# Convolution taps of a two-layer transformer block tied to the steps they are written between, and their shares of three stretches changed

## The chip, the cores and the metric

The kernel runs on one core of one Trainium2 chip. What counts is the device time of one launch in microseconds (us), the median of the runs. Line numbers (L1039) are those of the kernel before, unless a sentence says that they are of the changed kernel, where the same lines stand some 18 or 19 further down (L1039 is L1058 there).

## The reference

Two layers over 256 latent tokens and 256 context tokens of width 1024. Each layer: half a feed-forward step, four token mixers on one normalised input, merged by gates, and another half feed-forward step. The second layer updates the latent tokens alone (`update_ctx` is false), so its mixers' outputs have 256 tokens and not 512.

```python
def conv_module(u, conv_w, conv_b, ln_g, ln_b):           # branch B, 512 channels
    a, g = jnp.split(u, 2, axis=-1)
    y = a * jax.nn.sigmoid(g)
    y = lax.conv_general_dilated(y, conv_w[:, None, :], ..., feature_group_count=B_CH) + conv_b   # 31 taps
    return jax.nn.silu(layer_norm(y, ln_g, ln_b))

def merge(y_a, y_b, y_c, y_d, gate_logits, w_branch, w_out):
    y = jnp.stack([y_a, y_b, y_c, y_d], axis=2)
    proj = jnp.einsum('btnc,ncd->btnd', y, w_branch)
    g = jax.nn.sigmoid(gate_logits.reshape(gate_logits.shape[:2] + (N_BRANCH, D_MODEL)))
    return jnp.einsum('btnd,btnd->btd', g, proj) @ w_out

def token_mixing(n, nc, ...):
    aq, ak, av, bu, cq, ck, cv, du, gl = split_cols(n @ w_in)
    ...
    # A: attention with grouped keys, B: conv_module, C: attention as the difference of
    # two softmaxes per head, D: a two-dimensional Fourier transform
    y = merge(y_a, y_b, y_c, y_d, gl, w_branch, w_out)
```

## The kernel before

**Products.** All weights are fp32. Each product is made of three fp32r matmuls: a weight is cut into a high half (`hi`, rounded by ACT, L196) and a low half (`lo`, the difference, by DVE, L197), the activations likewise, and TensorE (PE) adds hi by high, hi by low and lo by high (`mm3`, L211 to L213; `mm3_rows` for products whose rows are tokens, L1355 to L1357 in the profile). Weights come in by DMA in chunks of 128x1024 (`raw`, three buffers), in the order in which the kernel asks for them, and the halves have three buffers each. PE is never without such work for long: the other engines must bring the halves and the activations in time.

**The mixing of a layer** is written as a list of main steps (most of them matmuls with weights) with side steps strewn between them. `spread(main, *sides)` (L95) runs the main steps in order and, behind each, as many steps of each side list as the share of the main steps' costs that is done. There are three such stretches, and then a closing one:

1. Fourier branch D, gates and projection of branch 3 (`gates_first`, which is `merge(3)`), channel block 2 of the convolution's input (`b_block(2)`), queries and keys of head 0 of branch C. Side steps: attention A (`side_a`), and the convolution taps up to `at1`.
2. Channel block 3 (`b_block(3)`), gates and projection of branch 0 (`merge(0)`). Side steps: the heads of branch C (`side_c`: scores, turn, norm, values, out), and the taps from `at1` to `at2`.
3. Gates and projection of branch 2 (`merge(2)`), which needs the heads of C. Side steps: the taps from `at2` on, and the convolution's end (`conv_tail`).
4. Gates and projection of branch 1, the convolution's (`merge(1)`), then the output projection.

**The taps.** The convolution has four blocks of 128 channels, each with a padded input `yp` and a sum `cv` (`cv0` to `cv3`). A block has 31 taps on DVE: the first sets `cv` (L1036), the other 30 each do cv = yp shifted * weight + cv (L1039). They stand in 44 side steps of up to three taps, eleven to a block (`nconv`). A tap handles 128x512 elements in the first layer (layer 0 below, `S` = 2), 128x256 in the second (layer 1, `S` = 1).

**The convolution's end** (`conv_tail`): the four sums added up (`cs`), PE's column mean of them (`cmean`, L1052), the mean subtracted on DVE (L1056), squares on ACT added on DVE, the root of the variance (`cln`: two small matmuls `cln_ps` with an ACT function between them), and for each block a product on DVE, a scaling on POOL (L1075), a tanh on ACT and the split into `yh` and `yl` (L237) that branch 1 multiplies.

**A branch's projection** (`b`) is multiplied by its gate on DVE (`bt`, L1386), and added to the running sum on POOL (`h`, L1388). The heads of branch C run on several engines in turn: PE scores, ACT exponentials, DVE sums and reciprocals (`stc`), the difference of the two softmaxes (`ec`, L1284), PE's turn of it (`tpc`, L1194), PE's values. The queries and keys of branch A pass a norm (`aq_w` on DVE, `aq_ps` on PE, L473 and L478).

**What sets the order.** Outside some regions with an order by hand, a scheduler sets each engine's order: it takes the instructions as they are written as a priority, and by its own model of durations puts an instruction onto an engine's queue when its data would be there. An instruction whose inputs are ready early may so stand far ahead of where it is written. The taps need only `yp`, the weights and their own `cv`, and DVE had room by that model: the taps of a block stand soon behind their `yp`, ahead of the steps between which they are written. On the queue, each engine then runs its instructions in that order. High and low halves of chunks have a higher priority than the rest (`high_priority`).

Of the kernel before, what the change touches and what calls it, by code (L numbers as in the profile page):

```python
# [24 lines left out]
TAPS = 31  # L25
# [66 lines left out]
    return 0.8 - 0.6 * math.exp(-0.3 * l)  # L92


def spread(main, *sides):  # L95

    total, at = sum(c for c, _ in main), 0.0
    done = [0] * len(sides)
    for c, step in main:
        step()  # L100
        at += c
        for i, side in enumerate(sides):
            upto = min(len(side), int(len(side) * at / total + 1e-6))
            for f in side[done[i]:upto]:
                f()
            done[i] = upto


def stepped(steps, costs):
# [18 lines left out]
class Build:  # L128
    def __init__(self, nc, tc, es, d):
        self.nc, self.tc, self.d = nc, tc, d  # L130
        self.order = []
        self.after = self.region = None
        self.level = False
        pool = lambda name, **kw: es.enter_context(tc.tile_pool(name=name, **kw))
        self.tiny = pool("tiny", bufs=1)
        self.fix = pool("fix", bufs=1)
        self.wp = pool("wp", bufs=3)
        self.tmp = pool("tmp", bufs=2)
        self.ps = pool("ps", bufs=1, space=PSUM)
        self.dram = pool("dram", bufs=1, space=bass.MemoryType.DRAM)  # L140
        f = self.fix
        for i in range(2):
            self.tiny.tile([128, 8], F32, tag="rs", name=f"rs{i}", bufs=2)
        self.tiny.tile([128, 1], F32, tag="warm", name="warm", bufs=1)
        self.lam = [f.tile([128, 4], F32, name=f"lam{l}") for l in range(L)]
        self.eps = f.tile([128, 1], F32, name="eps")
        self.small = f.tile([128, N_SMALL], F32, name="small")
        self.mod = [f.tile([128, 72, 2], F32, name=f"mod{l}") for l in range(L)]
        self.zero = f.tile([128, 32], F32, name="zero")[:, 0:1]
        self.const = f.tile([128, EARLY], F32, name="const")  # L150
        self.st = f.tile([128, DB, 32], F32, name="st")
        self.h = f.tile([128, DB, 2 * T], F32, name="h")
        self.nh = f.tile([128, DB, 2 * T], F32R, name="nh")
        self.nl = f.tile([128, DB, 2 * T], F32R, name="nl")

    def sm(self, *key):
        o, w = SMALL[key if len(key) > 1 else key[0]]
# [30 lines left out]
    def cut(self, r, low="vector", pool=None, bufs=3, into=None):  # L188
        i = len(self.order)
        with self.tc.high_priority():  # L190
            if into is None:
                hi, lo = ((pool or self.wp).tile([128, 8, 128], F32R, tag=n, name=f"{n}{i}", bufs=bufs) for n in ("hi", "lo"))
            else:
                hi, lo = (t.rearrange("p (a b) -> p a b", a=8) for t in into)
            hv, lv = (t.rearrange("p a b -> p (a b)") for t in (hi, lo))
            self.nc.scalar.activation(out=hv, in_=r, func=AF.Copy)  # L196
            getattr(self.nc, low).tensor_tensor(out=lv, in0=r, in1=hv.bitcast(F32), op=ALU.subtract)  # L197
        return Chunk(hi, lo)

    def chunk(self, desc):  # L200
# [775 lines left out]
    def mixing(self, l, closing):  # L976
# [5 lines left out]
        with self.tc.tile_pool(name=f"mix{l}", bufs=2) as mp:  # L982
# [48 lines left out]
            def taps(i, k0, k1):  # L1031
                o, yp = conv_out[i], pads[i]
                for k in range(k0, k1):
                    x, wk = yp[:, :, k:k + T], cw[:, i, k:k + 1]
                    if k == 0:
                        nc.vector.tensor_scalar(out=o, in0=x, scalar1=wk, scalar2=self.sm("conv_b", l)[:, i:i + 1],  # L1036
                                                op0=ALU.mult, op1=ALU.add)
                    else:
                        nc.vector.scalar_tensor_tensor(out=o, in0=x, scalar=wk, in1=o, op0=ALU.mult, op1=ALU.add)  # L1039
# [232 lines left out]
            def c_k(h):  # L1272
                p = win(C_K + 128 * h, 512, f"ck{h}")
                t = self.held(f"ckt{h}")
                nc.scalar.activation(out=t, in_=p, func=AF.Copy)
                rope(t)
                ck[h] = stack_k(t, f"ck{h}")
# [161 lines left out]
            def lagged(stages, extra):  # L1439
                side = []  # L1440
                lag = max(d for d, _ in stages)
                for i in range(n + lag):
                    side += extra.get(i, [])
                    for d, f in stages:
                        if 0 <= i - d < n:
# [5 lines left out]
                            {per * j - d: [lambda f=f, j=j: f(j)] for j in range(1, 4) for d, f in ((2, a_q), (1, a_q_turn))})  # L1451
            side_c = lagged([(3, c_out), (2, c_values), (2, c_norm), (1, c_turn), (0, c_scores)],
                            {per * h - 1: [lambda h=h: c_q(h), lambda h=h: c_k(h)] for h in range(1, 4)})
            conv = [lambda i=i, k=k: taps(i, k, min(k + 3, TAPS)) for i in range(4) for k in range(0, TAPS, 3)]
            nconv = len(conv) // 4
            conv_tail = [conv_sum, conv_mean, conv_rstd, conv_turn] + [lambda i=i: conv_norm(i) for i in range(4)]
            turn = a_k()
# [18 lines left out]
            def b_block(i):  # L1476
                return [(8, lambda: b_gate(i)), (8, lambda: b_value(i))]
# [6 lines left out]
            else:  # L1484
# [2 lines left out]
                cover = [lambda g=g: (f_columns(g + 1), steps[g]()) for g in range(3)] + [steps[3]]  # L1487
                gates_first.insert(2, gates_first.pop(0))
            fourier = [(8, lambda: f_columns(0))] + [four(g, cover[g]) for g in range(4)]
            at1, at2 = 2 * nconv + 2, 3 * nconv  # L1490
            spread(fourier + gates_first[:6] + b_block(2) + gates_first[6:] + [(8, lambda: c_q(0)), (8, lambda: c_k(0))],
                   side_a, conv[:at1])
            spread(b_block(3) + merge(0), side_c, conv[at1:at2])
            spread(merge(2), conv[at2:] + conv_tail)
            ready = []

            def cut_first(i):
# [119 lines left out]
```

## Time and profile before

| | us |
|---|---|
| runs | 2226.83, 2226.89, 2227.34: median 2226.89 |
| profiled execution, by its own clock | 2227.85 |
| its span in the profile | 2226.1 |
| granted TensorE clock, mean | 0.997 |
| POOL busy | 92.1 |

The profile is of one execution. Its span is what the rows below are parts of; the execution's own time is 1.75 us longer than the span, the median of the runs 0.8 us longer. Stretches of the span are named by their start and end in us. The two mixings' parts with taps are 417 to 870 (layer 0) and 1705 to 1990 (layer 1).

### The profile page before, as it was taken

How to read it: one execution, taken by the hardware profiler on the slowest of the kernel's cores; microseconds unless marked ns; L12 is line 12 of the kernel's file. 1: busy time of each engine (PE TensorE's matmuls, PEld its weight loads, DVE VectorE, ACT ScalarE, POOL GpSimd, SP SyncE). 2: the span in 40 equal slices, each digit the busy share in tenths (PEclk: the TensorE clock that was granted, in tenths of full speed). 3: DMA queues.
4: the chain of work that ended last, by engine and by line, in shares of the span. 5: the costliest groups of instructions: out<-in, count | busy, mean ns of one | idle time of the engine just before them, and what ended most of it. 6: DMA issues, size and time to landing. Idle time of an engine off the chain costs nothing. (4 is left out here: it accounts for less than half of the span.)

```text
span 2226.1 us, 30137 instructions
## 1 busy us (share of the span) xinstructions
PE 2194.1 (99%) x11700; PEld 1855.1 (83%) x11700; DVE 1486.3 (67%) x2456; ACT 995.0 (45%) x1611; POOL 92.1 (4%) x96
## 2 busy tenths in 40 slices
PE   7999999999999999999999999999999999999998
PEld 6888889888887788898888898888889987779887
DVE  5787775794779646555656545565647969877665
ACT  5322223466556634433222233332224778756553
POOL 0000000100000113010000010000001000020000
PEclk9999999999999999999999999999999999999999
DMA  8566664322222222424544423544543433465554
GB/s 330 188 202 200 204 210 137 118 72 67 76 73 71 82 98 95 133 97 160 157 158 149 168 97 124 169 151 162 167 144 137 133 124 107 139 220 167 191 181 151
DMA packets 90815, 323.15 MB, mean 145 GB/s; under 512 B 9904, under 2 KB 12208, under 8 KB 90032
## 3 DMA queue, kind: packets, MB, share of 16 engines
q1 hardware_dynamic: 90672, 321.22, 43.3%
q8 instruction: 92, 1.51, 0.3%
q14 instruction: 51, 0.42, 0.1%
HBM read 315.94 MB, written 5.24 MB: 144 GB/s over the span
## 5 line engine op out<-in xcount | busy, mean ns | idle before, releaser
L196 ACT ACTIVATE hi<-raw 128x1024 fp32r<-128x1024 f32 x419 | 443.4, 1059 | 796.4 <-PE p L212 239.0
L197 DVE TENSOR_TENSOR lo<-raw,hi 128x1024 fp32r<-128x1024 f32 x416 | 518.7, 1247 | 245.6 <-ACT hi L196 239.8
L424 DVE SCALAR_TENSOR_TENSOR prods<-raw,cond 128x1024 f32<-128x1024 f32 x240 | 288.9, 1222 | 229.5 <-DMA raw<-wst 229.4
L211 PE MATMUL p<-nh,hi 128*128 128x512 f32 (+1 forms) x1040 | 398.0, 383 | 0.0
L212 PE MATMUL p<-nl,hi 128*128 128x512 f32 (+1 forms) x1040 | 397.8, 383 | 0.0
L213 PE MATMUL p<-nh,lo 128*128 128x512 f32 (+1 forms) x1040 | 397.8, 382 | 0.0
L212 PEld LDWEIGHTS p<-nl,hi 128*128 128x128 f32 x1040 | 195.5, 188 | 38.2
L211 PEld LDWEIGHTS p<-nh,hi 128*128 128x128 f32 x1040 | 195.4, 188 | 38.2
L213 PEld LDWEIGHTS p<-nh,lo 128*128 128x128 f32 x1040 | 195.5, 188 | 37.5
L213 PE MATMUL pr<-gh,lo 128*128 128x512 f32 (+1 forms) x480 | 177.8, 370 | 0.0
L212 PE MATMUL pr<-gl,hi 128*128 128x512 f32 (+1 forms) x480 | 177.8, 370 | 0.0
L211 PE MATMUL pr<-gh,hi 128*128 128x512 f32 (+1 forms) x480 | 177.8, 370 | 0.0
L1039 DVE SCALAR_TENSOR_TENSOR cv<-yp,cw,cv 128x512 f32<-128x512 f32 (+1 forms) x240 | 148.1, 617 | 4.6
L219 PE MATMUL p<-nh,hi 128*128 128x512 f32 x304 | 107.5, 397 | 0.1
L211 PEld LDWEIGHTS pr<-gh,hi 128*128 128x128 f32 x480 | 90.4, 188 | 15.7
L213 PEld LDWEIGHTS pr<-gh,lo 128*128 128x128 f32 x480 | 90.4, 188 | 15.5
L212 PEld LDWEIGHTS pr<-gl,hi 128*128 128x128 f32 x480 | 90.4, 188 | 15.4
L211 PE MATMUL g<-nh,hi 128*128 128x512 f32 x256 | 101.2, 396 | 0.0
L213 PE MATMUL g<-nh,lo 128*128 128x512 f32 x256 | 100.4, 392 | 0.0
L212 PE MATMUL g<-nl,hi 128*128 128x512 f32 x256 | 100.1, 391 | 0.0
L233 ACT ACTIVATE gh<-s 128x512 fp32r<-128x512 f32 (+1 forms) x88 | 50.6, 575 | 97.7 <-DVE s L773 92.5
L220 PE MATMUL p<-nh,lo 128*128 128x256 f32 x304 | 85.5, 281 | 0.0
(510 smaller groups left out, 4164.5 us busy)
## 6 DMA issues: line engine op xcount, KB each, us to landing
raw<-wst SPq DMA_DIRECT2D x556, 512.0 KB, 3.4
adaraw<-wst SPq DMA_DIRECT2D x4, 2048.0 KB, 19.0
adaraw<-wst SPq DMA_DIRECT2D x8, 512.0 KB, 6.2
cond<-cond SPq DMA_DIRECT2D x3, 1024.0 KB, 6.1
h<-h SPq DMA_DIRECT2D x4, 512.0 KB, 5.3
parked<-h SPq DMA_DIRECT2D x8, 256.0 KB, 4.3
h<-parked SPq DMA_DIRECT2D x8, 256.0 KB, 3.5
late<-late SPq DMA_DIRECT2D x2, 608.0 KB, 5.8
```

The costliest lines, as they stand in the source:

```text
L196: self.nc.scalar.activation(out=hv, in_=r, func=AF.Copy)
L197: getattr(self.nc, low).tensor_tensor(out=lv, in0=r, in1=hv.bitcast(F32), op=ALU.subtract)
L211: mm(out, w[0], x[0], start=start, stop=False)
L212: mm(out, w[0], x[1], start=False, stop=False)
L213: mm(out, w[1], x[0], start=False, stop=stop)
L219: mm(out, w[0], self.nh[:, k], start=start, stop=False)
L220: mm(out[:, CTX], w[1], self.nh[:, k, LAT], start=False, stop=stop)
L233: nc.scalar.activation(out=hi, in_=src, func=AF.Copy, scale=scale)
L424: nc.vector.scalar_tensor_tensor(out=products[:, s], in0=r, scalar=1.0, in1=cond[:, s], op0=ALU.mult, op1=ALU.mult, accum_out=self.mod[l][ ...
L1039: nc.vector.scalar_tensor_tensor(out=o, in0=x, scalar=wk, in1=o, op0=ALU.mult, op1=ALU.add)
```

## The change

`spread` gets a callback, `then`, which runs behind each main step and its side steps. In the mixing it is `mark`: it notes the DVE instruction written last (low halves of chunks left aside, which are kept in `cuts`). Each side step of taps is now `held`: the first DVE instruction that it issues, its first tap, gets a dependency on the mark before the last, so that the scheduler may not put it ahead of that instruction on DVE's queue. Both stand on one engine, so the dependency makes no semaphore and no wait; it binds the scheduler alone. Taps behind the first of a block follow it by their own data.

The shares change too. Layer 0: `at1` stays at 24 steps, `at2` goes from 33 to 29, so that four more steps of taps are written in the third stretch. Layer 1: `at1` and `at2` are both 33, so that three blocks' taps are written in the first stretch and none in the second; the last block's eleven steps stay in the third. Eight empty steps (`late`) stand ahead of the taps in the first stretch, so that they begin later, and `b_block(2)`, whose output the third block's taps need, is written behind three of branch 3's remaining gate and projection steps, not six (`nb`).

```diff
-def spread(main, *sides):
+def spread(main, *sides, then=lambda: None):
...
             for f in side[done[i]:upto]:
                 f()
             done[i] = upto
+        then()
...
+    def mark(self):
+
+        for i in reversed(self.nc.cur_bb.bb.instructions):
+            if i.engine == E.DVE and i.name not in self.cuts:
+                return i
+
+    def behind(self, step, mark):
+
+        at = len(self.nc.cur_bb.bb.instructions)
+        step()
+        for i in self.nc.cur_bb.bb.instructions[at:]:
+            if i.engine == E.DVE:
+                kind = mybir.DependencyInfo(mybir.DependencyClass.NoSync, mybir.DependencyReason.DATA)
+                self.tc.add_manual_dep(i, mark.name, kind, reason="behind")
+                return
...
-            conv = [lambda i=i, k=k: taps(i, k, min(k + 3, TAPS)) for i in range(4) for k in range(0, TAPS, 3)]
+            marks = []
+
+            def held(i, k):
+
+                self.behind(lambda: taps(i, k, min(k + 3, TAPS)), marks[-2])
+
+            conv = [lambda i=i, k=k: held(i, k) for i in range(4) for k in range(0, TAPS, 3)]
+            mark = lambda: marks.append(self.mark())
...
-            at1, at2 = 2 * nconv + 2, 3 * nconv
-            spread(fourier + gates_first[:6] + b_block(2) + gates_first[6:] + [(8, lambda: c_q(0)), (8, lambda: c_k(0))],
-                   side_a, conv[:at1])
-            spread(b_block(3) + merge(0), side_c, conv[at1:at2])
-            spread(merge(2), conv[at2:] + conv_tail)
+            at1, at2 = (2 * nconv + 2, 2 * nconv + 7) if S == 2 else (3 * nconv, 3 * nconv)
+            late = [lambda: None] * (0 if S == 2 else 8)
+            nb = 6 if S == 2 else 3
+            mark()
+            mark()
+            spread(fourier + gates_first[:nb] + b_block(2) + gates_first[nb:] + [(8, lambda: c_q(0)), (8, lambda: c_k(0))],
+                   side_a, late + conv[:at1], then=mark)
+            spread(b_block(3) + merge(0), side_c, conv[at1:at2], then=mark)
+            spread(merge(2), conv[at2:] + conv_tail, then=mark)
```

Every engine issues the same computation as before; only places on the queues differ. A new order on DVE also shifts what the scheduler does on the other engines. Three places follow, as the two programs order them. In these rows L1181, L1039 and so on are lines of the program that the fence shows, and a number behind a name tells one buffer from another.

DVE, layer 1, second stretch: the chain of a head of branch C (`stc` the sums and reciprocals, `ec` the difference of the softmaxes, `lam` its factor, `lo` a chunk's low half). Before:

```order
L1181 TENSOR_REDUCE stc_15582<-sc_15579 128x1
L1181 TENSOR_REDUCE stc_15590<-sc_15587 128x1
L1039 SCALAR_TENSOR_TENSOR cv_13513<-yp_15229,cw,cv_13513 128x256
L1185 RECIPROCAL stc_15582<-stc_15582 128x1
L1039 SCALAR_TENSOR_TENSOR cv_13513<-yp_15229,cw,cv_13513 128x256
L1185 RECIPROCAL stc_15590<-stc_15590 128x1
L1039 SCALAR_TENSOR_TENSOR cv_13513<-yp_15229,cw,cv_13513 128x256
L1282 TENSOR_TENSOR stc_15590<-stc_15590,lam_76 128x1
L1039 SCALAR_TENSOR_TENSOR cv_13513<-yp_15229,cw,cv_13513 128x256 x2
L197 TENSOR_TENSOR lo_15769<-raw_15766,hi_15768 128x1024
L1284 SCALAR_TENSOR_TENSOR ec_15584<-ec_15584,stc_15582,ec_15592 128x512
```

Changed:

```order
L1200 TENSOR_REDUCE stc_15598<-sc_15595 128x1
L1200 TENSOR_REDUCE stc_15606<-sc_15603 128x1
L1204 RECIPROCAL stc_15598<-stc_15598 128x1
L1204 RECIPROCAL stc_15606<-stc_15606 128x1
L1301 TENSOR_TENSOR stc_15606<-stc_15606,lam_76 128x1
L215 TENSOR_TENSOR lo_15779<-raw_15776,hi_15778 128x1024
L1303 SCALAR_TENSOR_TENSOR ec_15600<-ec_15600,stc_15598,ec_15608 128x512
```

The five taps between the head's steps are gone. Of the 124 taps of layer 1, 93 now stand in the first stretch, none in the second and the last block's 31 in the third; there they stand in groups of one to six between the low halves, where before there was no tap.

DVE, layer 0, third stretch (`bt` a projection times its gate). Before:

```order
L1333 SCALAR_TENSOR_TENSOR bt_6792<-gt_6693,b_6779 128x512
L1333 SCALAR_TENSOR_TENSOR bt_6808<-gt_6729,b_6795 128x512
L197 TENSOR_TENSOR lo_6895<-raw_6892,hi_6894 128x1024
L197 TENSOR_TENSOR lo_6937<-raw_6934,hi_6936 128x1024
L197 TENSOR_TENSOR lo_6974<-raw_6971,hi_6973 128x1024
L1333 SCALAR_TENSOR_TENSOR bt_6911<-gt_6768,b_6898 128x512
L1333 SCALAR_TENSOR_TENSOR bt_6927<-gt_6848,b_6914 128x512
```

Changed:

```order
L1352 SCALAR_TENSOR_TENSOR bt_6783<-gt_6683,b_6770 128x512
L1058 SCALAR_TENSOR_TENSOR cv_3256<-yp_5428,cw,cv_3256 128x512 x3
L1352 SCALAR_TENSOR_TENSOR bt_6799<-gt_6719,b_6786 128x512
L215 TENSOR_TENSOR lo_6889<-raw_6886,hi_6888 128x1024
L1058 SCALAR_TENSOR_TENSOR cv_3256<-yp_5428,cw,cv_3256 128x512 x6
L215 TENSOR_TENSOR lo_6933<-raw_6930,hi_6932 128x1024
L1058 SCALAR_TENSOR_TENSOR cv_3256<-yp_5428,cw,cv_3256 128x512 x6
L215 TENSOR_TENSOR lo_6970<-raw_6967,hi_6969 128x1024
L1058 SCALAR_TENSOR_TENSOR cv_3256<-yp_5428,cw,cv_3256 128x512
L1352 SCALAR_TENSOR_TENSOR bt_6905<-gt_6758,b_6892 128x512
```

41 taps now stand in this stretch between its low halves and its `bt` steps. Further ahead in layer 0, the taps of block 0 no longer stand within the chain of the query norm (`aq`), but behind it.

PE, layer 1, the end of the third stretch and the start of the fourth (`g` the products of a gate, `b` of a branch, `ada` small products of the next step's modulation). Before, where branch 1 begins:

```order
L1356 MATMUL g_16354<-lo_16425,nh 128x512
L1357 MATMUL g_16354<-hi_16424,nl 128x512
L1355 MATMUL b_16461<-hi_16451,yh_16311 128x512
L1356 MATMUL b_16461<-lo_16452,yh_16311 128x512
L1357 MATMUL b_16461<-hi_16451,yl_16312 128x512
```

Changed, from the mean on, with the rows between left out of the second part:

```order
L1374 MATMUL g_16493<-hi_16497,nh 128x512
L1071 MATMUL cmean<-cs,const 128x256
L1374 MATMUL g_16494<-hi_16497,nh 128x512
L1375 MATMUL g_16493<-lo_16498,nh 128x512
L1376 MATMUL g_16493<-hi_16497,nl 128x512
```

```order
L421 MATMUL ada_16391<-adaraw_16396,st 32x256 x4
L421 MATMUL ada_16391<-adaraw_16402,st 32x256 x4
L1374 MATMUL g_16493<-hi_16545,nh 128x512
L1374 MATMUL g_16494<-hi_16545,nh 128x512
L1374 MATMUL b_16461<-hi_16451,yh_16311 128x512
L1375 MATMUL b_16461<-lo_16452,yh_16311 128x512
L1374 MATMUL b_16477<-hi_16451,yh_16311 128x512
L1375 MATMUL b_16477<-lo_16452,yh_16311 128x512
```

The mean stood 89 of PE's instructions ahead of the first product of branch 1, and stands 34 ahead now; in PE's queue it has moved 84 instructions back. Behind the mean, up to the product that reads the last block's `yh` or `yl`, stand 42 matmuls of 128x512 and 24 small `ada` ones, and among them the two steps of `cln_ps`.

More of the change, by code (lines that the diff above doesn't have):

```diff
@@ L133, in __init__ @@
         self.level = False
+        self.cuts = set()
         pool = lambda name, **kw: es.enter_context(tc.tile_pool(name=name, **kw))
@@ L196, in cut @@
             self.nc.scalar.activation(out=hv, in_=r, func=AF.Copy)
-            getattr(self.nc, low).tensor_tensor(out=lv, in0=r, in1=hv.bitcast(F32), op=ALU.subtract)
+            i = getattr(self.nc, low).tensor_tensor(out=lv, in0=r, in1=hv.bitcast(F32), op=ALU.subtract)
+            self.cuts.add(i.ins.name)
         return Chunk(hi, lo)
```

## The prediction

> **What bounds the kernel now.** I read the page's busy times first, then busy times by stretch of the two mixings, then who TensorE waited for there.
>
> ```profile
> PE 2194.1 (99%) x11700; PEld 1855.1 (83%) x11700; DVE 1486.3 (67%) x2456; ACT 995.0 (45%) x1611; POOL 92.1 (4%) x96
> ```
>
> TensorE (PE) is busy for 2194.1 of the 2226.1 us span, so only 32 us can be won without taking matmuls away, and the change takes none. The next rows tell where part of the 32 us lies. Layer 0 (the first mixing) is 417 to 870 us, layer 1 (the second) 1705 to 1990.
>
> ```profile
> 417.00:480.00 63.00, 62.01 (x294) 50.85 (x293) 60.00 (x94) 29.41 (x50) 0.18 (x2) 1.00 0.25 84
> 640.00:710.00 70.00, 69.33 (x345) 57.10 (x344) 64.67 (x127) 42.69 (x86) 3.61 (x2) 1.00 0.22 73
> 710.00:750.00 40.00, 37.77 (x191) 31.24 (x190) 26.23 (x53) 25.46 (x49) 3.96 (x2) 1.00 0.21 71
> 750.00:832.00 82.00, 81.66 (x390) 66.56 (x389) 40.97 (x63) 38.66 (x70) 11.24 (x8) 1.00 0.28 97
> 1705.00:1760.00 55.00, 55.00 (x349) 49.58 (x348) 49.34 (x102) 35.16 (x57) 0.15 (x2) 1.00 0.41 135
> 1760.00:1845.00 85.00, 84.87 (x587) 72.36 (x586) 65.97 (x137) 66.29 (x130) 0.16 (x2) 1.00 0.36 118
> 1845.00:1920.00 75.00, 70.23 (x373) 58.25 (x372) 71.89 (x154) 56.98 (x96) 2.54 (x2) 1.00 0.36 120
> 1920.00:1957.00 37.00, 35.15 (x175) 28.35 (x174) 26.38 (x42) 28.57 (x48) 6.54 (x4) 1.00 0.43 143
> 1957.00:1990.00 33.00, 31.86 (x159) 23.42 (x157) 24.43 (x38) 21.09 (x31) 10.32 (x8) 1.00 0.65 219
> ```
>
> The columns are stretch, length, then busy time of PE, weight loads, DVE (VectorE), ACT, POOL. The granted clock is 1.00 throughout. PE stands idle 4.8 us in 1845 to 1920 and 1.9 us behind it, and DVE is at 71.9 of 75 us there. In layer 0 it is 1.0 us at 417 to 480 (DVE 60 of 63) and 0.7 + 2.2 + 0.3 = 3.2 us from 640 to 832. The tail of layer 1, 1957 to 1990, has 1.1 us. The convolution taps (L1039) lie here:
>
> ```profile
> 417.00:480.00 63.00, 33.81 (x46) 1.00 0.25 84
> 640.00:710.00 70.00, 22.39 (x30) 1.00 0.22 73
> 750.00:832.00 82.00, 0.00 (x0) 1.00 0.28 97
> 1845.00:1920.00 75.00, 22.25 (x46) 1.00 0.36 120
> 1920.00:1957.00 37.00, 0.00 (x0) 1.00 0.43 143
> ```
>
> Where DVE is full, the taps are a third to a half of its work. Where it has room, none is left. Who PE waited for in 417 to 480, in 640 to 760 (one row) and in 1845 to 1930 (three):
>
> ```profile
> PE aq_ps L478 <- DVE aq_w L473: 0.8, 1, 0.8
> ...
> PE tpc L1194 <- DVE ec L1284: 2.2, 2, 1.2
> ...
> PE tpc L1194 <- DVE ec L1284: 2.6, 2, 1.9
> PE g L1355 <- ACT gt L1374: 2.0, 1, 2.0
> PE cs_ps L478 <- DVE cs_w L473: 1.7, 1, 1.7
> ```
>
> The gate wait is named after ACT, but ACT runs its queue in order, and in this stretch it had the scaling of a head's scores (needing DVE) ahead of the gates.
>
> **The change, part by part.** No instruction is added or taken away on any engine: a tap is told only which earlier DVE instruction it may not pass, on its own queue, so no new wait between engines. What changes is places. The prices, all from rows of one execution:
>
> ```profile
> 450.40 0.74 DVE L1039 SCALAR_TENSOR_TENSOR cv<-yp,cw,cv 128x512 f32<-128x512 f32 x1
> 452.18 1.54 DVE L1039 SCALAR_TENSOR_TENSOR cv<-yp,cw,cv 128x512 f32<-128x512 f32 x2
> 1712.12 1.00 DVE L1039 SCALAR_TENSOR_TENSOR cv<-yp,cw,cv 128x256 f32<-128x256 f32 x2
> 1889.22 1.22 DVE L197 TENSOR_TENSOR lo<-raw,hi 128x1024 fp32r<-128x1024 f32 x1
> 1890.36 0.74 DVE L1284 SCALAR_TENSOR_TENSOR ec<-ec,stc,ec 128x512 f32<-128x512 f32 x1
> 1893.25 2.54 POOL L1388 TENSOR_TENSOR h<-bt,h 128x512 f32<-128x512 f32 x2 [112.54 <-DVE bt L1386]
> 1894.88 1.19 DVE L1039 SCALAR_TENSOR_TENSOR cv<-yp,cw,cv 128x256 f32<-128x256 f32 x1
> 1896.11 0.49 DVE L1039 SCALAR_TENSOR_TENSOR cv<-yp,cw,cv 128x256 f32<-128x256 f32 x1
> ```
>
> A tap costs 0.74 to 0.77 us in layer 0 and 0.48 to 0.50 in layer 1. A chunk's low half (lo) costs 1.14 us from its start to the next start. A tap that meets an addition on POOL took 1.19 instead of 0.49: 0.7 us more.
>
> *Layer 1, second stretch.* The 46 taps of 1845 to 1920 go: some 18 into the first stretch, the rest to the third. DVE falls from 71.9 to 71.9 - 22.3 = 49.6 of 75 us. The heads' reduces, reciprocals and ec then stand behind one another instead of behind taps. The three kinds of wait lie on that queue or on ACT behind it. Of the 4.8 + 1.9 = 6.6 us I leave 1.0 for the two chains that are ACT's own (a table load of 1.28 us stands in each): **-5.6 us**. Bounds: 0, if the waits are ACT's, and -6.6.
>
> *Layer 0, first stretch.* The taps of the first channel block stood between the steps of the query norm that PE waited for. They go behind it. The idle 1.0 us goes: **-1.0** (0 to -1.0).
>
> *Layer 0, second stretch.* Some 30 taps leave 640 to 710, and DVE falls from 64.7 to about 43 of 70. But 2.2 of the 3.2 us idle lie in 710 to 750, where no tap stood and DVE was busy 26 of 40. They hang on lateness before 710 and on the chain itself. I take two thirds: **-2.1** (0 to -3.2).
>
> *Layer 0, third stretch.* 41 taps now stand here: 41 x 0.75 = 31 us onto 41.0 us in 82 makes 72, and the 8 additions of POOL hold DVE for another 8 x 0.7 = 5.6: 78 of 82. It fits barely, and the sum of the four blocks (cs) must be ready for PE's mean at 832. Cover: the two chunks by which the halves run ahead of PE. **+0.3** (0 to +5).
>
> *Layer 1, first stretch.* 115.3 us of DVE in 140 grow by 18 x 0.48 = 8.6 to 124: room remains, though not evenly: **+0.3** (0 to +3).
>
> *Layer 1, third stretch and tail.* All 31 taps of the last block stand in it: 26.4 + 31 x 0.48 = 41.3 us in 37. The program has moved PE's mean (cmean) 84 of its instructions back, some 17 us, whose share of the next stretch's chunk halves is about 8: 49 of 54 us, 51 with the additions. What is late next is the tail. These are its marks before:
>
> ```profile
> 1934.87 0.39 PE L1357 MATMUL g<-hi,nl 128*128 128x512 f32 x1
> ...
> 1939.18 0.40 PE L1355 MATMUL g<-hi,nh 128*128 128x512 f32 x1
> 1957.01 0.59 PE L1052 MATMUL cmean<-cs,const 128*128 128x256 f32 x2
> 1970.74 1.28 ACT L1078 ACT_TABLE_LOAD   x1
> 1971.49 4.56 POOL L1075 TENSOR_SCALAR cv<-cv,small 128x256 f32<-128x256 f32 x4 [2.65 <-DVE cv L1074]
> 1979.30 0.39 PE L1355 MATMUL b<-hi,yh 128*128 128x512 f32 x1
> 1983.19 0.42 DVE L237 SCALAR_TENSOR_TENSOR yl<-cv,yh 128x256 fp32r<-128x256 f32 x1
> ```
>
> The first two rows are 20 matmuls in a line: 4.31 / 19 = 0.227 us each. From the mean to the last piece that branch 1 reads took 1957.0 to 1983.6 = 26.6 us, and PE had 22.3 us of other work ahead of the branch. Now PE has some 42 matmuls x 0.227 = 9.5 us and 24 small ones of the modulation (I allow 1.5), 11 us in all, until it needs that last piece. The chain has shrunk too: three chunk halves stand in it on DVE instead of nine, 6 x 1.14 = 6.8 us less, so at its old pace it takes 19.8. Its own steps in a line (mean subtracted, squares, root with a table load, four products, POOL's four scalings, tanh, two splits) come to about 13.4 by my adding of their durations, an estimate. So PE waits 2.4 to 8.8 us against 1.1 idle before: +1.3 to +7.7. The steps are now written nearly back to back, so I take the near end: **+1.3**.
>
> Sum: -5.6 - 1.0 - 2.1 + 0.3 + 0.3 + 1.3 = -6.8. The profiled execution took 2227.85 us by its own clock, 2226.1 in span; the median of the runs is 2226.89, 0.8 over the span. 2226.1 - 6.8 + 0.8 = **2220.1**.
>
> [...] The row first: the tap at 1894.88 took 1.19 us, and the one after POOL's additions 0.49. [...] That the taps then stand among the additions in the third stretches is the second rival below.
>
> **The rivals.** *The waits stay* (0.20): PE's order was laid anew with DVE's, and a head's chain may be set by ACT. For it speak the 2.2 us idle in 710 to 750 without a tap. Against it, DVE at 96% where layer 1 waits. Then -5.6 becomes -2, -2.1 becomes -1: 2220.1 + 4.7 = 2224.8.
>
> *POOL's additions block the taps* (0.09): each addition (2.54 / 2 = 1.27 us) holds DVE whole while the taps follow one another at 0.77. In layer 0, 41.0 + 31.6 + 10.2 = 82.8 of 82 us; in layer 1, 49 + 4 x 1.27 = 54 of 54. Both sums come late by two or three us: +5, 2225.1. [...]
>
> *The tail is laid bare* (0.16), the one that ends slower: in layer 1 the last block's sum is late by 5 us on a DVE that is 94% full, and the chain keeps its old pace (+7.7). The gains of 8.7 less 0.6 stand against 12.7: 2226.1 + 4.6 + 0.8 = 2231.5. It decides from where the chain takes over 19 us. For it, the cover fell from 22 to about 8 us at the first product; against it, six halves fewer stand in its way.
>
> **How the numbers follow.** My forecast has 0.55, with a range of its own from 2214 (all waits gone: -6.6 - 1.0 - 3.2 - 1.1 = -11.9, 2215.0, and a little more) to 2224. The rivals have 0.20, 0.09 and 0.16. A measurement of this kernel tells about 0.2%, 4.5 us, from no change. Faster by more: 0.51 (the forecast but for its upper end). Within 0.2%: the first two rivals and that end, less a little: 0.32. Slower: the last rival, 0.16, and 0.01 of the second: 0.17. With the rivals taken in, the range is 2212 to 2231.
>
> **What would show it.** Right, if in the changed profile the head stretch of layer 1 (about 1845 to 1915) has no tap, DVE is near 50 of 75 us and PE idles under 1.5 us; if layer 0's query norm no longer makes PE wait; and if PE's wait before branch 1 in layer 1 (b on yh, or cln_ps) is about 3 us. Wrong, if PE still waits for ec or the gates with an idle DVE; if cmean waits for cs in either layer; or if b's wait for yh is over 8 us.

## The result, and the profile after

The changed kernel takes 2238.87 us (median of 4 runs, 2237.3 to 2240.06), the kernel before 2227.11 (4 runs): a ratio of 1.0052, 95% interval 1.0034 to 1.0069. It is 11.8 us slower. The forecast was 2220.1, with 2231 as the upper end of the range. The profiled execution of the changed kernel took 2237.3 us, the shortest of the four: the traces below account for a span that is 9.4 us longer, and not for the other 2 us or so of the medians' difference.

Busy times, first row of the page:

```profile
PE 2198.0 (98%) x11700; PEld 1855.1 (83%) x11700; DVE 1488.5 (67%) x2456; ACT 994.3 (44%) x1611; POOL 95.6 (4%) x96
```

PE is busy for 3.9 us longer with the same 11700 matmuls, so some of them ran slower. That is the first sign that not only waits were added.

Where the time went is read from the same instructions in both traces. Before (start, duration): the first turn of attention A in layer 1, the first and the last turn of branch C's heads, the last group of turns of the output's input (`zt`).

```profile
1758.65 0.60 PE L1194 MATMUL tpa<-const,ea 128*128 128x128 f32 x4
1855.10 0.60 PE L1194 MATMUL tpc<-const,ec 128*128 128x128 f32 x4
1939.41 0.60 PE L1194 MATMUL tpc<-const,ec 128*128 128x128 f32 x4
2008.48 0.82 PE L1404 MATMUL zt<-const,h 128*128 128x128 f32 x6
```

The changed kernel:

```profile
1755.18 0.60 PE L1213 MATMUL tpa<-const,ea 128*128 128x128 f32 x4
1854.20 0.63 PE L1213 MATMUL tpc<-const,ec 128*128 128x128 f32 x4
1935.58 0.60 PE L1213 MATMUL tpc<-const,ec 128*128 128x128 f32 x4
2018.26 0.82 PE L1423 MATMUL zt<-const,h 128*128 128x128 f32 x6
```

The changed kernel is ahead by 3.5 us at the first, by 0.9 at the second, by 3.8 at the third, and behind by 9.8 at the last. So attention A in the first stretch of layer 1 lost 2.6 us, the heads won 2.9, and the tail lost 13.6. The span grew by 9.4. The 3.5 us ahead of layer 1 are mostly scatter of the program's start: the kernel with layer 1 alone changed (below), in which nothing ahead of it differs, has the first of these instructions at

```profile
1756.38 0.60 PE L1213 MATMUL tpa<-const,ea 128*128 128x128 f32 x4
```

which is 2.3 us ahead as well. Layer 0 is left with about -1.2.

Stretches of the changed kernel (length; busy time of PE, weight loads, DVE, ACT, POOL; granted clock, share of DMA, GB/s):

```profile
415.00:478.00 63.00, 62.97 (x299) 51.91 (x298) 40.82 (x65) 30.41 (x52) 0.00 (x0) 1.00 0.24 84
748.00:830.00 82.00, 81.46 (x386) 65.75 (x385) 73.33 (x110) 37.87 (x68) 15.30 (x8) 1.00 0.27 91
...
1758.00:1845.00 87.00, 84.44 (x583) 71.64 (x582) 84.23 (x187) 65.70 (x130) 0.31 (x4) 1.00 0.34 115
1845.00:1920.00 75.00, 71.11 (x376) 58.61 (x375) 56.31 (x115) 59.77 (x104) 2.54 (x2) 1.00 0.36 120
1935.00:1950.00 15.00, 15.00 (x74) 11.81 (x73) 10.39 (x18) 10.73 (x14) 1.47 (x1) 1.00 0.56 182
1950.00:1977.00 27.00, 23.57 (x102) 18.58 (x100) 25.60 (x39) 12.43 (x14) 2.21 (x1) 0.99 0.59 197
1977.00:1990.00 13.00, 11.19 (x52) 6.61 (x53) 6.90 (x15) 5.36 (x9) 2.62 (x2) 0.63 0.44 155
```

Layer 0's query norm (first row) no longer holds PE up, and its third stretch bears its taps with DVE at 73 of 82 us. In layer 1 the first stretch now has the full DVE that the heads had before (84.2 of 87 us), and PE idle for 2.6 us. The heads have DVE at 56.3 of 75 us, and PE still idle for 3.9 (before: 4.8). The last three rows are the tail: DVE has 4.6 us of room, then none (25.6 of 27), and then the granted clock falls to 0.63 for 13 us.

Who PE waited for, in the first stretch, the heads and the tail:

```profile
PE tpa L1213 <- ACT ea L1208: 2.3, 2, 1.3
...
PE tpc L1213 <- DVE ec L1303: 2.7, 3, 1.7
...
PE g L1374 <- ACT hi L214: 4.7, 3, 2.5
PE zt L1423 <- POOL h L1407: 1.8, 1, 1.8
PE cmean L1071 <- DVE cs L1066: 0.7, 1, 0.7
```

The tail in order of time, one view by engine (start, duration, and in brackets the idle time ahead and what ended it):

```profile
1960.71 3.08 DVE L1058 SCALAR_TENSOR_TENSOR cv<-yp,cw,cv 128x256 f32<-128x256 f32 x6
...
1975.89 0.49 PE L1374 MATMUL g<-hi,nh 128*128 128x512 f32 x1 [2.55 <-ACT hi L214]
1976.62 0.42 DVE L1066 TENSOR_TENSOR cs<-cs,cv 128x256 f32<-128x256 f32 x1
1977.10 1.22 PE L1071 MATMUL cmean<-cs,const 128*128 128x256 f32 x2 [0.71 <-DVE cs L1066]
1978.54 0.63 PE L1375 MATMUL g<-lo,nh 128*128 128x512 f32 x1
1978.97 0.63 PE L1376 MATMUL g<-hi,nl 128*128 128x512 f32 x1
...
1983.10 1.06 ACT L214 ACTIVATE hi<-raw 128x1024 fp32r<-128x1024 f32 x1 [2.81 <-PE g L1376]
1984.18 1.22 DVE L215 TENSOR_TENSOR lo<-raw,hi 128x1024 fp32r<-128x1024 f32 x1 [2.55 <-ACT hi L214]
1984.20 0.73 PE L1374 MATMUL g<-hi,nh 128*128 128x512 f32 x2 [1.20 <-ACT hi L214]
```

Taps run in groups of up to six between low halves. The last sum (`cs`) is done at 1977.0, 20 us later than before. PE has run out of halves by then, since each low half stood behind taps, and a chunk's DMA may begin only when the low half made from its buffer is done. For the chunk that ends PE's wait at 1975.89, by the order of issues, a low half was done at 1970.56, the DMA issued at 1970.59, and the high half begun at 1974.79. PE stands idle from 1973.35 to 1977.1 but for one matmul. Behind it, the 128x512 matmuls start every 0.427 us (1978.54 to 1978.97) and no longer every 0.227.

Summed up from these rows and the single starts: waits up to the mean 2.7 + 1.0 = 3.7 us; slow matmuls, ten of 128x512 by 0.20, the mean, and seven groups of `ada` by 0.19, 3.6; a second wait for the next chunk's halves (1.6 + 0.7) 2.3; `ada` weights and halves that came late at 1992 to 1995, 1.8; the turns that wait for POOL's addition at 2004, 2.0. That is 13.4, against 13.6 lost. The sum is a rough one: the kernel before has 1.1 us of waits of its own in this stretch, and the changed kernel has eight more matmuls in it (one of a gate, seven of the output projection, about 1 us). The second wait has a cause of its own. There are three pairs of halves. Two of them lay filled for branch 1's products, which waited for the convolution, so the gate chunks ahead of it ran through one pair: PE's last use (1983.0), high half (1983.10), low half (1984.18), PE again.

### The profile page after: what moved, and what is told of

Its sections match the earlier page's. It is cut to its first block, busy times and chain, and to the rows that moved or that the text cites. A ratio compares the mean times of both kernels' runs of the same rounds, so it can differ in the third digit from the quotient of the medians.

```text
span 2235.5 us, 30128 instructions
## 1 busy us (share of the span) xinstructions
PE 2198.0 (98%) x11700; PEld 1855.1 (83%) x11700; DVE 1488.5 (67%) x2456; ACT 994.3 (44%) x1611; POOL 95.6 (4%) x96
## 5 line engine op out<-in xcount | busy, mean ns | idle before, releaser
L232 PEld LDWEIGHTS pr<-gh,lo 128*128 128x128 f32 x480 | 90.4, 188 | 15.3
```

The costliest lines, as they stand in the source:

```text
L232: mm(out, w[1], x[0], start=False, stop=stop)
```

## The experiments

The table counts layer 1's 124 taps by the program's order: ahead of the first difference of softmaxes (`ec`) of the heads, between the first and the last, and behind the last. Times are medians; the kernel before ran beside each group.

| run | taps ahead, among, behind | us | before, us | ratio (95%) |
|---|---|---|---|---|
| before | 82, 42, 0 | | | |
| changed | 93, 0, 31 | 2238.87 | 2227.11 | 1.0052 (1.0034 to 1.0069) |
| layer0_only | 82, 42, 0 | 2225.68 | 2226.72 | 0.9995 (0.9985 to 1.0004) |
| layer1_only | 93, 0, 31 | 2240.25 | 2226.72 | 1.0058 (1.0043 to 1.0072) |
| ties_only | 74, 19, 31 | 2229.27 | 2226.72 | 1.0012 (1.0002 to 1.0021) |
| shares_only | 93, 31, 0 | 2224.70 | 2226.72 | 0.9988 (0.9979 to 0.9998) |
| taps16 | 93, 0, 16 | 2229.01 | 2226.24 | 1.0009 (0.9999 to 1.0018) |
| repeat3 | 93, 0, 31 | 2240.22 | 2226.24 | 1.0064 (1.0047 to 1.0080) |
| l1_at2_38 | 93, 16, 15 | 2225.96 | 2226.24 | 0.9998 (0.9989 to 1.0007) |
| combo | 93, 31, 0 | 2224.04 | 2226.24 | 0.9987 (0.9978 to 0.9997) |
| loose5 | 93, 7, 24 | 2231.04 | 2227.48 | 1.0015 (1.0005 to 1.0024) |
| at1_24 | 74, 19, 31 | 2229.15 | 2227.48 | 1.0010 (1.0001 to 1.0020) |
| l1_at2_44 | 93, 31, 0 | 2225.47 | 2227.48 | 0.9992 (0.9982 to 1.0001) |
| g24_38 | 82, 42, 0 | 2224.92 | 2227.48 | 0.9990 (0.9981 to 1.0000) |
| stalls | 82, 42, 0 | 2275.76 | 2226.08 | 1.0223 (1.0193 to 1.0253) |
| stalls23 | 82, 42, 0 | 2286.53 | 2226.08 | 1.0271 (1.0242 to 1.0301) |

### Which layer, and which half of the change

layer0_only and layer1_only give the other layer its taps as before. The edit for layer0_only (layer1_only has (24, 33) for layer 0, the changed numbers for layer 1, and `held` where S is 1):

```diff
-            conv = [lambda i=i, k=k: held(i, k) for i in range(4) for k in range(0, TAPS, 3)]
+            conv = [lambda i=i, k=k: (held(i, k) if S == 2 else taps(i, k, min(k + 3, TAPS))) for i in range(4) for k in range(0, TAPS, 3)]
...
-            at1, at2 = (2 * nconv + 2, 2 * nconv + 7) if S == 2 else (3 * nconv, 3 * nconv)
-            late = [lambda: None] * (0 if S == 2 else 8)
-            nb = 6 if S == 2 else 3
+            at1, at2 = (24, 29) if S == 2 else (24, 33)
+            late = []
+            nb = 6
```

> Only layer 0 has the change (ties and shares); layer 1 has its taps as in the kernel before. Theory (the loss sits in layer 1's third stretch: 31 taps there fill DVE, the low halves come late, PE stands still and its clock is halved for some us; layer 0 changed by -0.3 us in the profile): 2226 to 2228 us. Rival (the ties cost wherever they are, layer 0's third stretch with its 41 taps too): 2230 to 2234 us.

> Only layer 1 has the change; layer 0 has its taps as before. Theory: all of the loss, 2237 to 2240 us, with PE's wait and a granted clock under 0.7 around 1975 to 1985. Rival (both layers share the loss): 2231 to 2235 us.

They measured 2225.68 and 2240.25. All of the loss is layer 1's; layer 0 may have won 1 us, which its interval does not tell from nothing. In layer1_only's trace, the wait ahead of the mean is 3.4 us, the clock is lowered three times from there on, and the tail loses 15.3 us: the loss differs by some us from one execution to another.

ties_only has the ties in both layers with the old shares (at1, at2 = 24, 33, no empty steps, block 2 behind six steps); shares_only has the new numbers with plain taps in place of `held`.

> The ties in both layers, but the shares, the place of channel block 2 and the start of the taps as in the kernel before. In the program's order this too puts 31 taps of layer 1 behind the heads, with 19 left among them. Theory (taps in the third stretch of layer 1 are the cause): 2233 to 2241 us, with a wait of PE and a lowered clock in that stretch again. Rival (the new shares, which empty the second stretch, are the cause): 2226 to 2229 us.

> The new shares, the later start and the moved channel block, without the ties. In the program's order no tap stands behind the heads in either layer, and 31 stand among them in both. Theory (taps behind the heads are the cause): 2225 to 2229 us, no lowered clock. Rival (the shares or the moved block are the cause): over 2233 us.

They measured 2229.27 and 2224.70. The shares alone do no harm: untied, the scheduler moved the last block's taps ahead again and left none in the tail. The ties alone cost 2.6 us, less than I expected of 31 taps behind the heads, and without a lowered clock in the tail. So their number alone does not settle the loss. The same two stretches of ties_only as of the changed kernel above:

```profile
1935.00:1950.00 15.00, 15.00 (x73) 11.63 (x72) 14.55 (x31) 9.17 (x15) 0.03 (x1) 1.00 0.64 211
1950.00:1977.00 27.00, 25.12 (x108) 19.66 (x106) 25.95 (x36) 15.08 (x20) 4.95 (x3) 1.00 0.60 192
```

DVE has no room left at 1935 to 1950 (14.55 of 15), where the changed kernel idles for 4.6 us. On the changed kernel's queue few taps stand there, ahead of steps that wait for PE or ACT; the rest come behind these steps, in the stretch that is full. DVE took its queue in order there, and a ready tap behind a waiting step did not fill the gap: in the changed kernel the last block's tap of 1937.63 was done at 1938.1, and the next one started at 1946.59, behind steps ahead of which DVE had stood idle for 1.21, 0.91, 0.38, 0.53 and 1.35 us. In ties_only PE's waits ahead of the mean and of `cln` are 1.5 and 1.2 us:

```profile
PE cmean L1071 <- DVE cs L1066: 1.5, 1, 1.5
PE cln_ps L486 <- DVE cs L1082: 1.2, 1, 1.2
```

### DVE's load against the order on PE

taps16 leaves out 15 of the last block's taps in layer 1:

```diff
-                for k in range(k0, k1):
+                for k in range(k0, min(k1, 16) if S == 1 and i == 3 else k1):
```

> The changed kernel with 15 of the 31 taps of layer 1's last block left out (the output is not the reference's), so that 16 taps stand in its third stretch: 15 x 0.5 = 7.5 us less work of DVE there, everything else as changed. Theory (DVE is full in that stretch, the low halves come late and PE starves): the wait of PE ahead of the mean and the lowered clock go, 2225 to 2231 us. Rival (the cause is the place of the mean and of the convolution's end on PE's queue, whatever DVE does): 2235 us or more.

It measured 2229.01, 9.9 us less than the changed kernel, for 15 taps of 0.5 us. The clock stays up:

```profile
1965.00:1977.00 12.00, 10.62 (x59) 7.83 (x59) 10.81 (x16) 9.18 (x12) 3.52 (x2) 1.00 0.55 195
1977.00:1990.00 13.00, 13.00 (x63) 9.61 (x62) 10.62 (x19) 7.78 (x14) 6.35 (x5) 1.00 0.68 256
```

The gain is larger than the work taken out (7.5 us), so the late taps set off something beyond themselves. 2.8 us over the kernel before stay, and by the rows used above its tail is still 2.7 us longer, with waits of 1.4 us each for `cs` and for `cln`. That these are what the order on PE costs with the load gone is likely, but no run isolates it; l1_at2_38 below has 15 taps there and `cmean` at 1954.4 in place of 1965.0, and its tail is only 0.4 us longer than before.

l1_at2_38 moves five steps of the last block into the second stretch (`at2` 38 in place of 33), l1_at2_44 all eleven (`at2` 44).

> The changed kernel with layer 1's at2 at 38 and not 33: five of the last block's eleven steps, 16 taps by the program's order, stand among the heads, and 15 behind them. Theory (too many taps in the third stretch): 2224 to 2230 us, no lowered clock, and at most 1 us more of waits in the heads. Rival (the ties as such spoil layer 1's order): 2233 us or more.

> The changed kernel with layer 1's at2 at 44: all 31 taps of the last block tied among the heads, none behind them. Theory: the tail costs nothing over before, the heads' waits come back in part (5 us where the changed kernel has 3.5 and 2.1 in 1875 to 1925): 2223 to 2228 us. Rival (ties among the heads hold them up): 2229 us or more.

2225.96 and 2225.47: with 15 taps behind the heads, or none, the tail's loss is gone, ties and all. The ties as such do not spoil the order.

loose5 keeps the shares, and ties the last block's steps to one mark three main steps ahead of the third stretch:

```diff
-                self.behind(lambda: taps(i, k, min(k + 3, TAPS)), marks[-2])
+                self.behind(lambda: taps(i, k, min(k + 3, TAPS)), marks[third[0] if third and S == 1 else -2])
...
+            third.append(len(marks) - 3)
             spread(merge(2), conv[at2:] + conv_tail, then=mark)
```

> The changed kernel with the same shares, but layer 1's last block tied less closely: all its steps of taps to the mark three main steps ahead of the third stretch, not each to its own. In the program's order 7 taps then stand among the heads and 24 behind them, and those begin sooner: eleven ahead of the stretch's first product with its gate, where the changed kernel has four. Theory (it is the lateness of the taps within the stretch: in the changed kernel DVE stood idle 4.6 us in 1935 to 1950 while taps were ready, and is full behind it): 2226 to 2230 us, no lowered clock. Rival (any two dozen taps there overfill the stretch): 2233 us or more.

2231.04: between the two theories. The clock was not lowered in the tail, and 7.8 us of the loss went, but not all: 24 taps there, begun early, still make PE wait in small pieces, and attention A's loss stays (4.2 us here, by the same two instructions as above). That is more than the 2.6 us of the changed kernel with the same waits, because here the clock was lowered behind them, from 1825.4 to 1828.8 us; in taps16 and l1_at2_44 as well.

at1_24 is the changed kernel with `at1` at 24 in layer 1.

> The changed kernel with layer 1's at1 at 24 as before, not 33; block place and later start as changed. By the program's order the third stretch then reads as in the kernel with ties alone. Theory (the larger share of the first stretch, by way of the scheduler's clock, puts the last block's taps late): 2227 to 2231 us. Rival (the moved block or the later start does it): 2235 us or more.

2229.15. The block's place and the later start are not it. With `at1` at 24, 19 taps stand among the heads, and the third stretch is ordered as in ties_only. How the first stretch's share comes to move the last block's taps within the third is the scheduler's doing; I read its result and did not take it apart.

### The lowered clock

repeat3 puts three products more (nine matmuls, 2.0 us) into the gate ahead of PE's long wait; they change that gate's sum:

```diff
+                        if S == 1 and br == 1 and f == 0 and t == 1 and k == DB - 1:
+                            for _ in range(3):
+                                mm3_rows(p, self.n(k, rows_of(t)), ch.wide(4 * (k - k2)), False, False)
                         mm3_rows(p, self.n(k, rows_of(t)), ch.wide(4 * (k - k2)), k == 0, k == DB - 1)
```

> The changed kernel with nine matmuls more (three products, 2.0 us) in the gate just ahead of PE's long wait in layer 1 (they are added to the gate's sum, which they change). PE is then busy where it stood idle for 2.55 us. Theory (the idle time itself lowers the granted clock): the clock stays at 1.00 from 1977 to 1990, the halved matmuls (12 x 0.2 us and the small ones) vanish, and 2.0 us more of work makes the kernel faster: 2233 to 2237 us. Rival (the clock is lowered by something else, or the slow matmuls were hidden by the late data anyway): 2239 us or more.

2240.22, and no answer: PE's wait was not filled but moved. The mean now waited for the last sum in one piece of 3.1 us, and the clock fell behind it as before (0.74 in 1977 to 1990):

```profile
1974.00:1978.00 4.00, 1.03 (x5) 0.57 (x4) 2.56 (x5) 1.49 (x2) 0.00 (x0) 1.00 0.65 183
1977.00:1990.00 13.00, 10.62 (x56) 6.95 (x57) 8.05 (x16) 6.04 (x10) 2.81 (x2) 0.74 0.34 116
```

So waits were made where nothing else is wrong. stalls and stalls23 are the kernel before, with waits in layer 0's feed-forward steps, where PE has no gap: a chain of copies on ACT from one product's sum, whose end writes into the next three products' sums, which PE then overwrites.

```diff
+            def stall(i, p, n):
+                t = self.temp(f"stall{i}")
+                nc.scalar.activation(out=t, in_=p, func=AF.Copy)
+                for _ in range(n - 1):
+                    nc.scalar.activation(out=t, in_=t, func=AF.Copy)
+                for key, bank in ((f"p1_{i + 1}", self.acc), (f"p3_{i + 1}", self.pair), (f"p1_{i + 2}", self.acc)):
+                    held[key] = bank(key)
+                    nc.scalar.activation(out=held[key][:, 0:8], in_=t[:, 0:8], func=AF.Copy)
```

> The kernel before with eight waits put into layer 0's two feed-forward steps, where PE has no gap: the next three products' sums are first written by the end of a chain of 1, 2, 3 and 4 (first step) and 2, 3, 4 and 6 (second) copies on ACT of about 0.6 us, so that PE stands still for about 1.5 to 5 us. The results are unchanged. Theory (idle time alone lowers the clock): up to about 1.9 us the next matmuls come at 0.227 us, over 2.7 us a dozen or more come at 0.427. Rival (the clock fell in the tail for another reason): 0.227 behind all of them.

> As above, with twelve waits of two and three copies (about 2 to 3 us), six in each step. Theory with a threshold by length alone: all waits of one length act alike, with one bound between 2.0 and 2.7 us. Theory with a window that runs freely: waits of one length between 2 and 3 us lower the clock in some places and not in others, and the stretch of slow matmuls has varied lengths.

The chains took longer than I had reckoned, so the twenty waits lie between 2.8 and 6.0 us, and none tests the range below. Behind 19 of the 20 the clock fell: 5 to 13 matmuls of 128x512 came at 0.427 us in place of 0.227, which is 1.0 to 2.6 us beside the wait. Idle time alone did it there. Granted clock behind one of the waits of stalls, and behind the longest:

```profile
1042.00:1045.50 3.50, 3.46 (x9) 2.76 (x10) 1.45 (x3) 0.81 (x3) 0.00 (x0) 0.56 0.39 152
...
1194.60:1199.00 4.40, 4.40 (x10) 3.48 (x11) 0.00 (x0) 0.14 (x2) 0.00 (x0) 0.50 0.33 119
```

Two waits of stalls23 of one length (2.67 in brackets for both, 2.83 from start to start less the usual pace, as the lengths in this part are counted), one with a fall of the clock and one without, and for each the windows around its end, each 3.41 us long:

```profile
125.84 0.50 PE L214 MATMUL p<-nh,hi 128*128 128x512 f32 x1 [2.67 <-ACT p L780]
163.04 0.50 PE L214 MATMUL p<-nh,hi 128*128 128x512 f32 x1 [2.67 <-ACT p L780]
...
123.70:127.11 3.41, 1.27 (x6) 1.06 (x7) 2.66 (x4) 2.25 (x7) 0.00 (x0) 1.00 0.30 117
127.11:130.52 3.41, 3.41 (x10) 2.64 (x9) 2.60 (x5) 0.63 (x1) 0.00 (x0) 0.50 0.67 217
...
161.25:164.66 3.41, 1.62 (x7) 1.34 (x8) 3.41 (x5) 2.54 (x8) 0.00 (x0) 1.00 0.35 120
164.66:168.07 3.41, 3.41 (x17) 2.80 (x16) 1.41 (x4) 0.00 (x0) 0.00 (x0) 1.00 0.76 259
```

In the first, five matmuls still come at the old pace before it halves. Length alone did not decide, then; where the wait lay in time did too. The traces show how. Within a trace, all changes of the granted clock lie whole multiples of 3.41 us apart (in the changed kernel's tail they are at 1976.26, 1983.09, 1986.50 and 1989.91), and the windows above are cut at these times. The first wait left PE idle for 2.14 us of its window (3.41 less 1.27), the second for 1.79, because its beginning fell into the window before. Between 60 and 2200 us of the sixteen traces, 32 such windows at the full clock have 2.0 us or more of PE's idle time, and the clock was halved in the next one behind all 32. Of those with 1.87 us or less, three were followed by half the clock (1.64 to 1.75 us idle), all in tails where the clock had been lowered less than 4 us before. No wait here had to fill a window: 2.0 us of idle time in one were enough.

### Versions meant to be better than both

combo is layer 0 as changed, and layer 1 with the new shares untied. g24_38 ties layer 1's taps too, with at1 at 24 and at2 at 38, and block and start as before.

> Layer 0 as changed, layer 1 with the new shares and block place but without the ties (no tap behind its heads). From the runs before: layer 0 alone gave 2225.7, the shares without ties 2224.7, before 2226.7. If both gains are real and add up: 2222 to 2225 us. If they are one and the same scatter: 2225 to 2227 us.

> Meant as the better version: layer 0 as changed; layer 1 with ties, but at1 24, block place and start as before (so without the 2.6 us wait for attention A at 1821 of the changed kernel), and at2 at 38. By the program's order 42 taps stand among the heads and none behind them. Theory: 2222 to 2226 us. Rival (the heads wait for the taps as in the kernel before): 2226 to 2228 us.

2224.04 and 2224.92. combo is 2.2 us (0.13%, 0.03 to 0.23%) faster than the kernel before, shares_only about as much (0.12%). Both are at the edge of what can be told, and so is whether layer 0's change adds anything. g24_38's interval reaches to no change at all. No version tried gained more.

## Why the prediction was wrong

**Layer 1, third stretch and tail (+1.3): the step that failed.** It measured +13.6. The place was right, and the rival "the tail is laid bare" had about its size, 5 + 7.7 = 12.7 us, though made up of other parts, so that the nearness is chance. Three readings of mine were at fault.

First, the sum "49 of 54 us" treats the stretch as one bin. DVE worked in order, and in 1935 to 1950 it stood idle for 4.6 us in front of steps that were not ready. The 5 us that the sum left over were that idle time, and the rest of the stretch was full.

Second, I took PE's other work as cover of 11 us. It was no cover: the halves for that work come from the same DVE, behind the same taps, and later through one pair of buffers while two were held for branch 1. PE ran out of halves even before the mean.

Third, I priced a wait by its length. A wait of 2.7 us just ahead of the mean also halved the clock (0.50 from 1976.3 to 1983.1), for some 3.6 us more. In the mixings of the kernel before no wait shows that (the longest is 2.2 us, with a clock of 1.00). But its trace does show it at the start of the program, where PE waits several times for its first data, and 128x512 matmuls behind that start every 0.43 us:

```profile
22.70:29.50 6.80, 5.83 (x69) 4.78 (x70) 2.59 (x7) 1.06 (x1) 0.00 (x0) 0.50 1.03 422
```

So the trace of the kernel before did show that the clock fell behind waits; the sum left it out.

How much each part of the tail is worth by itself is settled only in part. With the same 31 taps begun earlier, as in at1_24, the tail loses 4.3 us (the last row of turns, against the last turn of the heads, in both traces) and the clock stays up. So some 9 of the 13.6 us hang on the taps' lateness within the stretch, with the clock's 3.6 among them. What the scheduler would have to know to place them better was not tried.

**Layer 1, second stretch (-5.6).** It measured -2.9. The taps left and DVE fell to 56.3 of 75 us (49.6 forecast, the stretch being ordered anew). PE's wait at 1888 stayed (1.9 us for `ec`; 2.2 before, named after a gate). DVE was idle for 0.9, 0.5 and 0.6 us from 1885.6 on, waiting for ACT, and then one low half stood ahead of `ec`. That is the first rival, the waits stay, for about half of the sum. That a head's chain through PE, ACT and DVE sets them fits these rows; no run tests it.

**Layer 1, first stretch (+0.3).** It measured +2.6, within its bound of +3. The 82 taps in 1758 to 1845 fill DVE as they had filled it in the heads, and attention A waits. This row group shows it: eight taps in a line, then the sum that the scaling on ACT needs, which PE's turn at 1822 and 1824 waits for.

```profile
1815.80 3.25 DVE L1058 SCALAR_TENSOR_TENSOR cv<-yp,cw,cv 128x256 f32<-128x256 f32 x8
1818.97 0.69 DVE L1200 TENSOR_REDUCE sta<-sa 128x1 f32<-128x512 f32 x1
...
1821.09 0.16 DVE L1204 RECIPROCAL sta<-sta 128x1 f32<-128x1 f32 x1
```

l1_at2_44, where the tail is whole, still has this loss; g24_38, which has fewer taps ahead of the heads, does not. The number alone does not make it: shares_only has the same 93 taps ahead, untied, and loses only 0.4 us there. So with the ties, part of the heads' waits was moved, not removed.

**Layer 0.** The query norm (-1.0) was right: PE is busy for 62.97 of 63 us there. The heads (-2.1) gave about -0.8 (PE idle for 2.9 us before in 640 to 750, for 2.1 in the same stretch of the changed kernel). The third stretch (+0.3) cost about 0.2, and DVE's 73.3 of 82 us is under my 78. The 46 taps there took 39.02 us, 0.85 each against 0.75 for one alone, so some 4.5 us went to meetings with POOL's additions: eight taps overlap one, and five of them took 1.66 to 1.79 us, all the others 0.73 to 0.75. The additions took 1.9 us each in place of 1.4. "POOL's additions block the taps" is thus a real effect, though the rival counted 8 x 1.27 = 10.2 us, with DVE held whole through each addition, which no run shows. It cost PE nothing here, since DVE had room.

The forecast's own test, that b's wait for `yh` would be about 3 us, missed the place: PE never waited for `yh` for long in the changed kernel; its waits lay ahead of that. Two of the signs that it gave for being wrong came true: `cmean` waited for `cs` (0.7 us), and PE still waited for `ec` in the heads (2.7 us).

## What to carry to other kernels

A filler does not fill an engine's gaps by itself: DVE, which ran its queue in order, stood idle for 4.6 us of 1935 to 1950 with ready taps behind the waiting steps. So a stretch is to be checked by its parts, not by busy time against length. When work is moved away from a full stretch, look at where it is full next, and at whether the "other work" that is to cover a late chain is fed by the same engine. A wait of TensorE that grew from under 2 to about 3 us cost more than its length here: behind 22 of the 23 waits of 2.7 us and more, 5 to 13 matmuls of 128x512 came at 0.427 us in place of 0.227. Short waits were cheaper than one long one only where they lay apart: two of 1.0 and 1.3 us of idle time, less than 1 us apart, halved the clock in three of seven traces.

## What the runs showed of the hardware

The price of a wait, from the traces of all these kernels: of the waits of 2.7 us and more, 22 of 23 were followed by 5 to 13 matmuls at half pace; of the 19 from 2.0 to 2.3 us, eight, with two to seven slow 128x512 matmuls. Of shorter ones, a pair of 1.2 and 1.5 us close together was in three of seven traces, and in two tails a wait of 1.4 to 1.6 us behind a clock just lowered; no other was. What decided was the sum of idle time in a window of 3.41 us: from 2.0 us on, the next window ran at half the clock, 32 times of 32. This fits that a wait of about 2.2 us, at the same place in the heads, lowered the clock in some executions and not in others.

The fall came up to 1.4 us after the wait's end (2.2 in repeat3, where a short wait followed the long one), and the clock was back to full within 6 us in steady work (in stalls it reads 0.50 in 1194.6 to 1199, behind its longest wait, and 0.95 in 1199 to 1204). In the changed kernel it was low twice, from 1976.3 to 1983.1 behind the wait ahead of the mean, and from 1986.5 to 1989.9 behind the second wait of 1.6 us. The clock that the profile grants is a mean over the window asked for, so windows must be cut to some microseconds to see this: over the whole span it reads 0.997 for both kernels.
